# Toeplitz weights of a state-space layer, copied on GpSimd into contiguous columns before the products load them

## The chip, the cores and the metric

The kernel runs on one core of one Trainium2 chip. The metric is the device time of one execution in microseconds (us). The engines are named as in the profile: PE is TensorE (matrix products), PEld its weight loads, DVE is VectorE, ACT is ScalarE, POOL is GpSimd, SP is SyncE, which here only issues transfers.

## The reference, cut to what matters

One layer of a hybrid decoder for 512 prompt positions and 8 sample tokens. The part that the change touches is the state-space mixer: 32 groups of 16 channels, each with 64 complex states.

```python
bu = jnp.einsum('bcgi,gpi->bcgp', u_c, b_bar)            # inputs into the states
_, local = lax.associative_scan(combine, (a, bu), axis=1)  # s[t] = lam_bar * s[t-1] + bu[t]
s_all = local + decay[None] * s[:, None]
y = jnp.einsum('bcgp,gip->bcgi', s_all, c_mat).real      # states out to the channels
...
y = y.reshape(bsz, t, D_SSM) + ssm_d * u_f
out = z * sigmoid(z @ w_glu)                              # z = gelu(y)
```

Around it stand the modulation (`w_ada`), the input projection (`w_in`), three attention branches, the output projection (`w_out`) and an MLP of width 4096. All of it is float32.

## The kernel before, in words

The kernel writes the scan in steps of 8 positions. Within a step the output of a group is a lower triangular block Toeplitz product of its inputs (8 positions x 16 channels = 128 rows); across the 64 steps it is a scan over the carried state. The loop `for qd in range(8)` handles a **quad** of 4 groups at a time:

- `BP`, `Cb` (DVE) are the powers of lambda times B and C. `pm0` (L766, PE) is the 16-column kernel of each group, copied to `M0` (L768, DVE; the trace calls these `pm` and `M`).
- `M0` is written to DRAM (`mscr`, L772) and read back with overlapping rows as the Toeplitz block `Tz` (L774), a tile of [128, 8, 16, 4]: position, channel and, innermost, the group. The columns of one group so lie 4 floats (16 bytes) apart. Both transfers are issued by SP.
- `pvs` (L792, PE) takes the inputs into the states; `Vs`, `Vp` (ACT), `W`, the scan `Rr` (L803, DVE) and `Rp` (ACT) lead to `Sx` (DVE and two small POOL memsets, L808 and L813). `rho` (L785) is the scan's decay, copied on POOL.
- `py` (named `pys`) adds two products for each group: one with weights `Tz` (L819) and one with weights `Cb` (L820).

```python
for g in range(GQ):
    c = slice(g * 80, (g + 1) * 80)
    nc.tensor.matmul(py[:, c], Tz[:, :, :, g].rearrange("p t c -> p (t c)"), U[:, qd * GQ + g], start=True, stop=False)
    nc.tensor.matmul(py[:, c], Cb[:, g].rearrange("p t c -> p (t c)"), Sx[:, g, 0:80], start=False, stop=True)
```

A float32 product of this kind appears as two records (two passes) in the trace, so 32 products of a line are 64 records.

All tiles of the loop have one buffer. Beside the loop stand other products, which the same stretch holds: the compressed keys of the samples (`turned`: `pxc`, `xc`; `compressed`: `ph`, `pk`, `php`), the modulation (`pada`, `padt`) and the key and value projections (`pkv`). A scheduler sets the order of instructions on every engine from a model of their durations; each engine then works through its own list strictly in order. So a change of one instruction can move others, also far behind it. The attention stage that follows (`pst` scores, `pe` exponentials, `ptp` and `PT` transposes, `po` values; `rslc` gathered cache rows, `pkT`, `ktS`, `poS` for the samples) is ordered in the same way; there `w_out` (`wo`) is loaded and split by ACT (L63) and DVE (L64).

Of the kernel before, what the change touches and what calls it, by code (L numbers as in the profile page):

```python
# [9 lines left out]
F32 = mybir.dt.float32  # L10
# [6 lines left out]
P = 128  # L17
# [19 lines left out]
def body(tc, i, o, dbg=None):  # L37
    nc = tc.nc
# [18 lines left out]
    def pst(tag, name):  # L57
        return bank["tile"].tile([P, 512], F32, tag=tag, name=name, bufs=bank["tags"][tag])
# [154 lines left out]
    GQ = 4  # L213
# [271 lines left out]
    def cmul(outr, outi, ar_, ai_, br_, bi_, tmp):  # L485
        nc.vector.tensor_tensor(outr, ar_, br_, ALU.mult)
        nc.vector.tensor_tensor(tmp, ai_, bi_, ALU.mult)
        nc.vector.tensor_tensor(outr, outr, tmp, ALU.subtract)
        nc.vector.tensor_tensor(outi, ar_, bi_, ALU.mult)
        nc.vector.tensor_tensor(tmp, ai_, br_, ALU.mult)  # L490
        nc.vector.tensor_tensor(outi, outi, tmp, ALU.add)
# [102 lines left out]
    sl = slx.enter_context(tc.tile_pool(name="sl", bufs=1, reuse_waits="tile"))  # L594
    xTp = sl.tile([P, 2, 2, 8, 32], F32, name="xTp")
    U = sl.tile([P, NG, 80], F32, name="U")
# [130 lines left out]
    for qd in range(NG // GQ):  # L727
# [43 lines left out]
        Tz = sl.tile([P, 8, 16, GQ], F32, tag="Tz", name="Tz")  # L771
        nc.sync.dma_start(mscr[qd, 112:240], M0.rearrange("p c g -> p (c g)"))  # L772
        mw = mscr[qd, 0:P]
        nc.sync.dma_start(Tz, bass.AP(tensor=mw.tensor, offset=mw.offset, ap=[[GQ * 16, P], [16 * GQ * 16, 8], [1, GQ * 16]]))  # L774

        CT = sl.tile([P, GQ, 8, 8], F32, tag="CT", name="CT")
        ST = sl.tile([P, GQ, 8, 8], F32, tag="ST", name="ST")
        tq = sl.tile([P, GQ, 8, 8], F32, tag="tq", name="tq")
        b8 = [P, GQ, 8, 8]
        ab = [tab[:, x, 1, gs].unsqueeze(3).to_broadcast(b8) for x in range(2)] + [tab[:, x, 0, gs].unsqueeze(2).to_broadcast(b8) for x in range(2)]  # L780
        cmul(CT, ST, *ab, tq)
        CT = CT.rearrange("p g a b -> p g (a b)")
        ST = ST.rearrange("p g a b -> p g (a b)")
# [14 lines left out]
        W2 = sl.tile([P, GQ, 64], F32, tag="W2", name="W2")  # L798
        nc.vector.tensor_tensor(W, Vs[:, :, 0:64], CT, ALU.mult)
        nc.vector.tensor_tensor(W2, Vp, ST, ALU.mult)  # L800
# [8 lines left out]
        nc.vector.tensor_tensor(W2, Rp, ST, ALU.mult)  # L809
        nc.vector.tensor_tensor(W, Rr, CT, ALU.mult)  # L810
        nc.vector.tensor_tensor(Sx[:, :, 1:65], W, W2, ALU.subtract)
# [4 lines left out]
        py = pst("ss", "pys")  # L816
        for g in range(GQ):
            c = slice(g * 80, (g + 1) * 80)
            nc.tensor.matmul(py[:, c], Tz[:, :, :, g].rearrange("p t c -> p (t c)"), U[:, qd * GQ + g], start=True, stop=False)  # L819
            nc.tensor.matmul(py[:, c], Cb[:, g].rearrange("p t c -> p (t c)"), Sx[:, g, 0:80], start=False, stop=True)  # L820
        nc.scalar.copy(ys.rearrange("p g c -> p (g c)"), py[:, 0 : GQ * 80])
        nc.sync.dma_start(yscr[qd], ys)
# [482 lines left out]
    for n in range(16):  # L1305
# [6 lines left out]
        if n % 4 == 3:  # L1312
            nc.tensor.matmul(po, Vbd[:, j // 2, 2 * (j % 2) : 2 * (j % 2) + 2].rearrange("p h d -> p (h d)"), etc[:, j // 2], start=False,
                             stop=True)
# [265 lines left out]
```

## Time and profile before

| | |
|---|---|
| times of three runs, us | 912.84, 912.87, 920.48 (median 912.87) |
| the profiled execution, us | 918.94; its span 917.2 |
| PE busy, share of the span | 95% |
| DVE, ACT, POOL busy | 58%, 42%, 7% |
| state-space loop in the span | about 133 to 264 us |
| attention | about 265 to 456 us |
| output projection and MLP | from about 456 us to the end |

The busy share of PE is made of modelled ends, so the rows are read by the starts of instructions that follow each other. The profiled execution is 6.07 us above the median of the three runs; a term worked out from it is taken off either.

### The profile page before, as it was taken

How to read it: one execution, taken by the hardware profiler on the slowest of the kernel's cores; microseconds unless marked ns; L12 is line 12 of the kernel's file. 1: busy time of each engine (PE TensorE's matmuls, PEld its weight loads, DVE VectorE, ACT ScalarE, POOL GpSimd, SP SyncE). 2: the span in 40 equal slices, each digit the busy share in tenths (PEclk: the TensorE clock that was granted, in tenths of full speed). 3: DMA queues.
4: the chain of work that ended last, by engine and by line, in shares of the span. 5: the costliest groups of instructions: out<-in, count | busy, mean ns of one | idle time of the engine just before them, and what ended most of it. 6: DMA issues, size and time to landing. Idle time of an engine off the chain costs nothing.

```text
span 917.2 us, 16412 instructions
## 1 busy us (share of the span) xinstructions
PE 869.2 (95%) x6517; PEld 759.1 (83%) x6517; DVE 527.5 (58%) x1413; ACT 388.7 (42%) x880; POOL 65.1 (7%) x147
## 2 busy tenths in 40 slices
PE   2899999999999999997999999999999999999995
PEld 1667997788998566655669989999999999999995
DVE  5776564758847865565659875443333444434534
ACT  1555325534435655454646544442111344433322
POOL 6001101000144100000000000000000000000000
PEclk9999997999999999997999999999999999999998
DMA  8957587366465352104154572233332222332302
GB/s 290 322 173 246 188 149 216 116 207 192 119 205 170 106 183 92 40 8 184 43 189 134 188 231 66 95 87 91 94 90 92 91 93 93 88 97 80 93 1 94
DMA packets 111836, 122.36 MB, mean 133 GB/s; under 512 B 24500, under 2 KB 91880, under 8 KB 109584
## 3 DMA queue, kind: packets, MB, share of 16 engines
q1 hardware_dynamic: 102256, 89.71, 32.2%
q0 software_dynamic: 5488, 29.99, 9.6%
q10 hardware_dynamic: 4016, 1.62, 0.7%
q8 instruction: 51, 0.84, 0.4%
q14 instruction: 25, 0.20, 0.1%
HBM read 112.47 MB, written 13.03 MB: 137 GB/s over the span
## 4 chain that ended last, share of the span: by engine, by line
PE 87%; DMA 7%; ACT 3%; DVE 2%; issue 1%; SPq 0%; ACTq 0%
PE pdn L1385 20%; PE pup L1385 20%; PE pj L605 5%; PE pkv L647 5%; PE pwo L1385 5%; PE ph L387 5%; DMA wada<-w_ada 4%; PE po L1244 4%; PE pada L334 2%; PE ptp L1239 2%; PE pg L1261 2%; PE pys L819 2%; PE pst L1211 1%; PE pS L1032 1%; PE pkT L1023 1%; PE pst L1212 1%
## 5 line engine op out<-in xcount | busy, mean ns | idle before, releaser
L1385 PE MATMUL pdn<-hidL,wH 128*128 128x256 f32 (+1 forms) x480 | 136.1, 284 | 0.0
L1385 PE MATMUL pdn<-hidH,wL 128*128 128x256 f32 (+1 forms) x480 | 135.9, 283 | 0.0
L1385 PE MATMUL pdn<-hidH,wH 128*128 128x256 f32 (+1 forms) x480 | 135.4, 282 | 0.0
L1385 PE MATMUL pup<-h2H,wL 128*128 128x256 f32 (+1 forms) x480 | 135.0, 282 | 0.0
L1385 PE MATMUL pup<-h2L,wH 128*128 128x256 f32 (+1 forms) x480 | 135.0, 282 | 0.0
L1385 PE MATMUL pup<-h2H,wH 128*128 128x256 f32 (+1 forms) x480 | 134.1, 283 | 0.0
L1385 PEld LDWEIGHTS pup<-h2L,wH 128*128 128x128 f32 x480 | 90.4, 188 | 0.8 <-DVE rs_t L97 0.8
L1385 PEld LDWEIGHTS pdn<-hidH,wL 128*128 128x128 f32 x480 | 90.6, 189 | 0.0
L1385 PEld LDWEIGHTS pdn<-hidL,wH 128*128 128x128 f32 x480 | 90.4, 188 | 0.1
L1385 PEld LDWEIGHTS pup<-h2H,wL 128*128 128x128 f32 x480 | 90.4, 188 | 0.0
L1385 PEld LDWEIGHTS pdn<-hidH,wH 128*128 128x128 f32 x480 | 90.4, 188 | 0.0
L1385 PEld LDWEIGHTS pup<-h2H,wH 128*128 128x128 f32 x480 | 89.6, 188 | 0.0
L63 ACT CAST wH<-wdn 128x1024 fp32r<-128x1024 f32 x30 | 31.5, 1050 | 114.0 <-PE pdn L1385 104.2
L64 DVE TENSOR_TENSOR wL<-wup,wH 128x1024 fp32r<-128x1024 f32 x30 | 36.7, 1225 | 58.1 <-ACT wH L63 58.1
L64 DVE TENSOR_TENSOR wL<-wdn,wH 128x1024 fp32r<-128x1024 f32 x30 | 36.8, 1225 | 54.2 <-ACT wH L63 54.2
L387 PE MATMUL ph<-xc,w 128*128 128x256 f32 (+2 forms) x320 | 66.4, 360 | 0.7 <-DVE xc L377 0.7
L387 PEld LDWEIGHTS ph<-xc,w 128*128 128x128 f32 x320 | 53.7, 206 | 11.7 <-issue 5.7
L63 ACT CAST wH<-wup 128x1024 fp32r<-128x1024 f32 x30 | 31.5, 1050 | 48.3 <-PE pup L1385 37.6
L1244 PE MATMUL po<-PT,Vx 128*64 128x512 f32 (+3 forms) x128 | 43.9, 450 | 1.5 <-ACT PT L1242 1.5
L1217 DVE TENSOR_REDUCE mxa<-pst 128x1 f32<-128x512 f32 (+1 forms) x64 | 29.7, 486 | 27.1 <-PE pst L1213 27.0
L1463 ACT ACTIVATE rl<-pup 128x256 f32<-128x256 f32 (+1 forms) x64 | 24.4, 384 | 48.9 <-PE pup L1385 48.8
L375 ACT COPY xc<-pxc 64x256 f32<-64x256 f32 x96 | 32.1, 366 | 25.1 <-DVE xc L377 18.6
(557 smaller groups left out, 2032.5 us busy)
## 6 DMA issues: line engine op xcount, KB each, us to landing
wada<-w_ada SPq DMA_DIRECT2D x20, 1024.0 KB
wup<-w_up SPq DMA_DIRECT2D x16, 1024.0 KB
wdn<-w_down SPq DMA_DIRECT2D x16, 1024.0 KB
wo<-w_out SPq DMA_DIRECT2D x8, 1024.0 KB
wada<-w_ada SPq DMA_DIRECT2D x8, 512.0 KB
rwin<-state_win SPq DMA_DIRECT2D x4, 1024.0 KB
new_win_sample<-state_win POOLq DMA_DIRECT2D x2, 2044.0 KB, 8.4
wkv<-w_in SPq DMA_DIRECT2D x3, 1024.0 KB
```

The lines of the kernel that those rows point to most:

```text
L63: nc.scalar.copy(h, src)
L64: nc.vector.tensor_tensor(l, src, h, ALU.subtract)
L334: nc.tensor.matmul(ps[k % 4 * 32 : k % 4 * 32 + 32], cT[:, k], rs[k // kp][:, k % kp], start=(k < 4), stop=(k >= 4))
L375: nc.scalar.copy(dst[:, :, :, hf], srcv[:, :, :, hf])
L387: nc.tensor.matmul(phv[:, lo:hi, 0:w], w1[n][:, r_], xc[n][:, lo:hi, r_ % 8, off : off + w], start=(r_ == 0), stop=(r_ == 15))
L605: nc.tensor.matmul(ps[:, 0:HB], w[:, k], x[:, k, hc], start=(k == 0 and n == 0), stop=(k == KT - 1 and n == 2))
L647: nc.tensor.matmul(ps[0:mp, 0:nw], x[:, k, tok], w[:, k % 4], start=(k == 0 and n == 0), stop=(k == KT - 1 and n == 2))
L819: nc.tensor.matmul(py[:, c], Tz[:, :, :, g].rearrange("p t c -> p (t c)"), U[:, qd * GQ + g], start=True, stop=False)
L1217: nc.vector.tensor_reduce(mx[:, qt : qt + 1], d, AX.X, ALU.max, negate=True)
L1244: nc.tensor.matmul(po[hh * 64 : hh * 64 + 64, kt * P : T], Vx[:, kt, kb], PT[:, c0 : c0 + T - kt * P], start=(br == 0 and kt == 0), stop=F ...
L1385: nc.tensor.matmul(ps[:, 0 : b - a], w, x[:, a:b], start=first and n == 0, stop=last and n == 2)
L1463: nc.scalar.activation(rl, ps[:, 0 : b - a], AF.Relu)
```

## The change: what it does, and the diff

A new tile `Tc` of [128, 4, 128] holds the four blocks of a quad one behind the other. One POOL copy of 512 elements in each of 128 partitions fills it from `Tz`, and the products take their weights from `Tc`. Nothing is removed.

```diff
         nc.sync.dma_start(Tz, bass.AP(tensor=mw.tensor, offset=mw.offset, ap=[[GQ * 16, P], [16 * GQ * 16, 8], [1, GQ * 16]]))
 
+        Tc = sl.tile([P, GQ, P], F32, tag="Tc", name="Tc")
+        nc.gpsimd.tensor_copy(Tc, Tz.rearrange("p t c g -> p g (t c)"))
+
...
         for g in range(GQ):
             c = slice(g * 80, (g + 1) * 80)
-            nc.tensor.matmul(py[:, c], Tz[:, :, :, g].rearrange("p t c -> p (t c)"), U[:, qd * GQ + g], start=True, stop=False)
+            nc.tensor.matmul(py[:, c], Tc[:, g], U[:, qd * GQ + g], start=True, stop=False)
```

In the changed kernel the lines behind L775 stand three lower (L819 is L822, L820 is L823, L785 is L788); the copy is L777.

The scheduler's order changes with it, from the first `pys` to the end of attention; the output projection and the MLP keep theirs. Three places follow.

POOL, from the `xc` memset (between the first and the second quad) on, before:

```order
L356 MEMSET xc 128x16x4
L785 COPY rho<-rh_133 128x256
L786 MEMSET rho 128x4
L813 MEMSET Sx 128x4x8
L808 MEMSET Sx 128x4
```

And after:

```order
L356 MEMSET xc 128x16x4
L777 COPY Tc<-Tz 128x512
L788 COPY rho<-rh_133 128x256
L789 MEMSET rho 128x4
L816 MEMSET Sx 128x4x8
L811 MEMSET Sx 128x4
```

The copy of each quad stands ahead of the next quad's `rho` copy and of this quad's `Sx` memset, so both wait until `Tz` has landed and been copied.

PE, from the last product of the first quad to the first Toeplitz product of the second, before (`w_155` and `w_156` are the two halves of the compression weights, `pm_1644`, `pm_1646` and so on a quad's `pm0`):

```order
L820 MATMUL pys<-Sx,Cb 128x80
L792 MATMUL pvs<-U,Bb 128x72 x4
L387 MATMUL ph<-xc,w_155 128x2x128 x7
L387 MATMUL ph<-xc,w_156 128x2x128 x6
L819 MATMUL pys<-U,Tz 128x80
```

And after:

```order
L823 MATMUL pys<-Sx,Cb 128x80
L766 MATMUL pm_1646<-C_136,BP 128x16 x4
L387 MATMUL ph<-xc,w_155 128x2x128 x5
L387 MATMUL ph<-xc,w_156 128x2x128 x3
L767 MATMUL pbb<-ident,BP 128x128 x4
L387 MATMUL ph<-xc,w_156 128x2x128 x11
L795 MATMUL pvs<-U,Bb 128x72 x4
L387 MATMUL ph<-xc,w_156 128x2x128
L822 MATMUL pys<-U,Tc 128x80
```

The second quad's `pm0`, which before stood ahead of these rows, behind the first Toeplitz product, has moved into this piece: 4 `pm`, 20 `ph`, 4 `pbb` and 4 `pvs` now lie between it and the product that needs its block.

ACT, in attention, from a value copy to the score exponentials, before:

```order
L1050 COPY ptS<-ppt 128x512 x2
L1221 ACTIVATE pe,dn<-pst,mxa 128x512
L1125 ACTIVATE ovS<-poS,sdn 128x128
L1270 COPY bcr<-bc 128x512
L1271 COPY bcr<-bs 128x8
L63 CAST wH<-wo 128x1024 x2
L1221 ACTIVATE pe,dn<-pst,mxa 128x128
```

And after:

```order
L1053 COPY ptS<-ppt 128x512 x2
L1245 COPY PT<-ptp 128x512 x2
L1128 ACTIVATE ovS<-poS,sdn 128x128
L1245 COPY PT<-ptp 128x256
L1224 ACTIVATE pe,dn<-pst,mxa 128x512
L63 CAST wH<-wo 128x1024
L1273 COPY bcr<-bc 128x512
```

The cast of `wo` stands a few rows earlier among the copies, and still ahead of the next exponentials.

## Rows read from the trace of the kernel before

**Rows 1.** Busy time by stage: stretch; its us; PE, PEld, DVE, ACT, POOL busy; clock.

```profile
144.00:265.00 121.00, 120.43 (x821) 107.34 (x820) 82.99 (x224) 52.07 (x141) 13.29 (x40) 0.96 0.53 164
265.00:417.00 152.00, 149.61 (x983) 101.23 (x981) 95.92 (x282) 81.30 (x218) 24.02 (x55) 1.00 0.33 108
417.00:426.00 9.00, 2.95 (x17) 2.39 (x17) 6.21 (x12) 3.89 (x9) 0.93 (x1) 0.68 0.90 345
```

**Rows 2.** The chain of waits from 140 to 270 us, by line (cut by the view).

```profile
by line: PE ph L387 22.5%; PE pkv L647 22.4%; PE pys L819 10.6%; PE pada L334 6.6%; PE php L697 5.5%; PE pys L820 5.4%; PE pm L766 4.3%; DMA wada<-w_ada 4.2%; PE pxc L368 4.1%; PE pvs L792 4.0%; ACT xc L375 3.5%; PE pbb L767 2.7%; PE padt L
```

**Rows 3.** The instructions of `pys`: ns minimum/median/maximum, first and last start, form.

```profile
L819 PEld LDWEIGHTS pys<-U,Tz x64: 308/326/337, 144.4 to 262.5; 128*128 128x128 f32 x64
L820 PEld LDWEIGHTS pys<-Sx,Cb x64: 187/190/208, 154.0 to 262.9; 128*128 128x128 f32 x64
```

**Rows 4.** PE in order of time, first quad: start, us, line, operation.

```profile
154.38 0.63 PE L819 MATMUL pys<-U,Tz 128*128 128x80 f32 x2
154.84 0.39 PE L820 MATMUL pys<-Sx,Cb 128*128 128x80 f32 x2
155.06 0.63 PE L819 MATMUL pys<-U,Tz 128*128 128x80 f32 x2
```

**Rows 5.** PE, a quad's first Toeplitz product and what follows, twice.

```profile
162.99 0.48 PE L819 MATMUL pys<-U,Tz 128*128 128x80 f32 x2
163.30 4.52 PE L387 MATMUL ph<-xc,w 128*128 128x256 f32 x20
...
177.06 0.64 PE L819 MATMUL pys<-U,Tz 128*128 128x80 f32 x2
177.53 1.04 PE L368 MATMUL pxc<-ident,rc 128*128 128x128 f32 x8
```

**Rows 6.** POOL in order of time: a memset of 512 elements and `rho` copies of 256.

```profile
95.12 0.54 POOL L719 MEMSET U<- 128x512 f32 x1
96.27 0.40 POOL L785 COPY rho<-rh 128x256 f32<-128x256 f32 x1 [0.60 <-DVE hL L201]
...
228.29 2.07 POOL L785 COPY rho<-rh 128x256 f32<-128x256 f32 x1 [5.99 <-DVE Rr L803]
```

**Rows 7.** DVE in order of time, beside the last of these copies.

```profile
228.35 0.42 DVE L810 TENSOR_TENSOR W<-Rr,CT 128x256 f32<-128x256 f32 x1
...
229.69 0.42 DVE L488 TENSOR_TENSOR CT<-CT,tq 128x256 f32<-128x256 f32 x1
230.02 0.30 DVE L341 TENSOR_REDUCE mod<-padt 128x36 f32<-128x144 f32 x1
```

**Rows 8.** SP's issues of the block's two transfers.

```profile
168.91 0.33 SPq L772 DMA_DIRECT2D mscr<-M  x1
172.25 0.37 SPq L774 DMA_DIRECT2D Tz<-mscr  x1
...
236.26 0.37 SPq L774 DMA_DIRECT2D Tz<-mscr  x1
```

**Rows 9.** PE in order of time: the product behind the last of these, and a row of `ph`.

```profile
157.32 5.82 PE L387 MATMUL ph<-xc,w 128*128 128x256 f32 x26
...
240.92 0.57 PE L819 MATMUL pys<-U,Tz 128*128 128x80 f32 x2
```

**Rows 10.** DVE in order of time, behind the end of a quad's `pys`.

```profile
156.64 0.69 DVE L757 TENSOR_TENSOR Cb<-lr,C 128x512 f32<-128x512 f32 x1 [6.05 <-PE pys L820]
...
157.36 0.69 DVE L759 TENSOR_TENSOR Cb<-Cb,tmp 128x512 f32<-128x512 f32 x1
```

**Rows 11.** The stop in attention, in order of time: transfer, ACT, PE.

```profile
415.66 11.52 SPq L1401 DMA_DIRECT2D wo<-w_out  x2
...
422.75 1.99 ACT L63 CAST wH<-wo 128x1024 fp32r<-128x1024 f32 x2 [5.11 <-DMA wo<-w_out]
...
425.71 0.80 PE L1211 MATMUL pst<-KH,QS 128*128 128x512 f32 x1 [4.02 <-ACT pe L1221]
```

**Rows 12.** PE's other wait of that stretch, 400 to 456 us: us in total, times, longest.

```profile
PE pkT L1023 <- DVE Os L1066: 2.0, 1, 2.0
```

## The prediction

> **What bounds the kernel now.** I read the windows by stage first. Through the state-space loop PE is busy for 120.43 of 121.00 us [rows 1], so it has half a microsecond of idle time there, while DVE, ACT and POOL each have 38 us or more to spare. The chain of waits says the same from the other side: from 140 to 270 us it runs through PE's lines, one behind the other, with transfers at 4.2% and ACT's copies at 3.5% [rows 2]. In such a stretch a shorter PE instruction is worth its own shortening, as long as PE finds its next operand ready. Two shares of that row belong to the edit: the 32 products with `Tz` hold 10.6%, the 32 with `Cb` 5.4%. They have the same shape (128x128 weights, 80 moving columns) and differ in how the weights lie. In attention PE is nearly full as well (149.61 of 152.00 us), but then comes a hole: 2.95 us of work in the 9 us from 417, with the granted clock at 0.68, a mean of its two levels of 2.4 and 1.2 GHz [rows 1]. That hole matters because the change re-orders the instructions around it.
>
> **Removed: the strided weight loads.** A load from `Tz` takes 326 ns, one from `Cb` 190 [rows 3]. Loads overlap with products, so I price by starts. A `Tz` product is followed after 0.46 us (154.38 to 154.84), a `Cb` product after 0.22 (154.84 to 155.06) [rows 4]. Within a quad three of four Toeplitz products stand between `Cb` products: 24 in all, and with contiguous weights each should move at `Cb`'s pace: 24 x (0.46 - 0.22) = 5.8 us. The first product of each quad is followed by something else after 0.31 to 0.47 us [rows 5]; at the middle, 0.39, that is 8 x (0.39 - 0.22) = 1.4 us. Sum 7.2. The chain gives nearly the same: 10.6% less 5.4% of 130 us is 6.8 us [rows 2]. Bounds: 5.8 if the firsts gain nothing, and 64 x 0.136 = 8.7 if each record's whole excess counts [rows 3]. I take 7.0, between the two ways of counting.
>
> **Added: eight copies on POOL.** The trace has no POOL copy of 512 elements or of this stride. Nearest are a memset of 512, 0.54 us, and the `rho` copy of 256, 0.40 [rows 6]. Undisturbed, the new copy is bounded by 0.54 below (a write of as many elements) and, with twice the `rho` copy raised by the stride's factor on PE (326/190 = 1.7), by 1.4 above. I take 0.8, twice `rho`. It can also be held up: the `rho` copy at 228.29 took 2.07 us, and in that time DVE ran one two-input operation after another from 228.35 until a one-input reduction at 230.02 [rows 6, 7]. So a POOL copy that meets such a train can lose 1.7 us; the new one would then take 2.5, or 4.1 if it stretched in proportion. The Trainium skill, "SBUF — State Buffer", section "Who interferes with whom", says that a DVE instruction with two SBUF inputs contends with a GpSimd instruction that reads SBUF, and that the later one waits; these rows agree, and by that rule a copy could also hold up DVE for its own length. By its own 0.8 us that would be 6.4 us of DVE time in eight quads, which DVE has.
>
> None of this is PE time; the question is whether PE has other work until `Tc` is ready. PE does, by its list: after the first quad the next Toeplitz product stands behind 4 `pm`, 20 `ph`, 4 `pbb` and 4 `pvs`. A `ph` record is 5.82/26 = 0.22 us and each `ph` has two, so the `ph` alone cover 9.0 us [rows 9]; the 12 others hold 4.3, 2.7 and 4.0% of the chain's 130 us for eight quads, 1.8 us in one [rows 2]. Cover: 10.8. Against it stands the chain of the block, which in this quad starts late: behind the end of `pys` DVE has two operations on `Cb` and one on `Sx`, from 156.64 to 158.05, 1.4 us [rows 10], and I allow 0.4 (an estimate: a little over half of one 0.69 us operation, for a copy of an eighth of the elements) for `M0` and the way to `mscr`. From the issue of `mscr` to that of `Tz` 3.34 us pass [rows 8]; `Tz` has landed at most 4.66 us after its issue, since the product at 240.92 did not wait [rows 8, 9]. With the copy of 0.8: 1.4 + 0.4 + 3.3 + 4.7 + 0.8 = 10.6, just under the cover; with a copy of 2.5 it is 12.3, over it by 1.5; at 4.1 by 3.1. This is the tightest quad: in the others more rows lie between `pm` and the product. I take 0.5 us of new waiting for this quad and 0.5 for the other seven together, with bounds of 0 and 8 x 3.1 = 25 us.
>
> **Queues that the copy stands in.** POOL's list is in order: while the copy waits for `Tz`, the next quad's `rho` and this quad's `Sx` memset wait with it. `rho` is needed by the next scan, a whole quad later; the `Sx` memset feeds the `Cb` products, which stand behind the Toeplitz product anyway. So I price this at nothing. If the block came later than the scan's result, the memset would be late by the same amount as `Tc`, a wait already counted. In exchange `Tz` is free once it is copied, not once PE is done with it, so SP can issue the next read earlier; a gain of slack, not of time.
>
> **Moved: everything up to 456 us.** The re-ordering keeps the instructions, and PE's own work with it; what can change is where PE waits. The one large stop is at 417 to 426: `wo` is issued at 415.66, lands at 422.75, and ACT, whose next instruction is its cast, stands still for 5.11 us; behind the cast wait the exponentials, and PE stops for 4.0 and 2.0 us [rows 11, 12]. In the new order the cast still stands ahead of the next exponentials, with a few more copies done before it. So I expect the stop to stay: 0, with bounds of -6 (both waits gone; a little more with the clock) and +6 (another such stop).
>
> **The sum.** -7.0 + 1.0 + 0 = -6.0 us. On the profiled execution: 918.94 - 6.0 = 912.9. It is 6.07 above the median of the runs shown, so against the median of 912.87 the forecast is 906.9. Its own range, from the bounds of the loads and half of attention's either way, is 901 to 911.
>
> **The rivals.** *(a) The stop in attention shrinks too.* For: ACT has more copies behind it when it reaches the cast, so PE has more to do meanwhile. Against: `wo` waits for the same buffer and shares its transfer time with two gathers. With both waits gone: -7 + 1 - 6 = -12, 900.9; from -3 on it is faster by over 1%.
>
> *(b) PE waits for the copy in every quad.* Mechanism: DVE's two-input trains hold up the POOL copy (2.07 us instead of 0.40, [rows 6, 7]), at each `Tc`, and PE reaches the product first. It needs a copy of over 1.0 us in the second quad (cover 10.8, chain 9.8 without the copy) and as little cover in the others. At copies of 4.1 us, 3.1 of waiting in each quad: +25 - 7 = +18, 930.9. From 0.9 us a quad on the gain is eaten, from 2.0 on it is slower by over 1%. For: DVE is busy for 83 of 121 us [rows 1], mostly with such operations. Against: only one of eight `rho` copies shows it at this size, and later quads have more cover.
>
> *(c) The load does not follow the stride.* Then the weights from `Tc` load no faster, and -7.0 falls away: 912.87 + 1.0 = 913.9. For it: the 326 ns could belong to something else about `Tz`. Against: `Cb`'s loads, of the same shape and in the same stretch, never go above 208, and `Tz`'s never below 308 [rows 3]. The Trainium skill, "TensorE: Matmul & The Clock Gate", section "LDWEIGHTS (loading the stationary operand)", has the load's time follow from its columns alone, 128 / 1.2 = 107 ns, without a term for stride; by that rule the change saves nothing, and the two medians for the same 128 columns speak against it.
>
> *(d) The new order makes another stop in attention:* +6 - 6 = 0, 912.9.
>
> **How the numbers follow.** Forecast 0.55, (a) 0.20, (b) 0.08, (c) 0.06, (d) 0.11. One per cent (9.1 us) is about what a measurement of this kernel can tell from no change. Faster by over 1% (below 903.7): all of (a) but a quarter, and a little over a fifth of the forecast's own range, 0.15 + 0.12 = 0.27. Slower by over 1%: (b), with 0.01 for a larger stop in (d), 0.09. The rest, 0.64, is within 1%. For 8 in 10 the range reaches from most of (a), 898, to past (c) and (d), 917; (b) is left out above and the end of (a) below.
>
> **What would show it.** Right: loads of `pys` from `Tc` at about 190 ns, `Tc` products followed after 0.22 us, PE idle under 2 us in the loop, POOL copies at 0.6 to 1.4 us with a few longer. Wrong: a wait of PE for POOL at L822, or, behind 265 us, a stop that is new or gone, which would be the larger part of the difference.

## The result, and the profile after

The changed kernel takes 927.65 us (median of 4 runs, 925.1 to 928.6) and the kernel before 914.16 beside it (4 runs). The ratio is 1.0137, 95% interval 1.0099 to 1.0175: 13.5 us slower, where 6 us faster was forecast. The profiled execution took 928.6 us. Two of all the executions timed below, one of e10 at 969.37 us and one of the kernel before at 1407.8 us beside e13, ran at a much lower granted clock (0.847 and 0.562) and stand in no median or ratio here. Of the changed kernel's page, the span, and busy time and instructions by engine:

```profile
span 926.9 us, 16416 instructions
PE 869.2 (94%) x6517; PEld 750.0 (81%) x6517; DVE 534.3 (58%) x1413; ACT 388.2 (42%) x880; POOL 75.9 (8%) x155
```

PE is busy for as long as before, 869.2 us, though its weight loads have become cheaper: the sum also holds products that ran at the lower clock and so took longer, and does not show the saving. Busy time and clock by stage, as in [rows 1], with attention cut where it now stops:

```profile
144.00:265.00 121.00, 116.00 (x841) 99.11 (x839) 89.53 (x224) 52.53 (x143) 17.76 (x38) 0.99 0.52 158
265.00:327.00 62.00, 59.01 (x399) 42.58 (x396) 43.79 (x120) 33.32 (x89) 25.39 (x58) 1.00 0.56 181
327.00:340.00 13.00, 6.21 (x26) 5.09 (x25) 3.94 (x10) 2.37 (x6) 0.00 (x0) 0.74 0.48 158
340.00:417.00 77.00, 76.54 (x416) 46.03 (x415) 41.89 (x125) 39.59 (x110) 2.86 (x3) 1.00 0.12 42
417.00:440.00 23.00, 19.81 (x159) 13.63 (x159) 14.15 (x45) 8.76 (x21) 1.88 (x2) 0.85 0.50 183
```

Two things are new: 5.0 us of idle PE time in the loop (0.57 before), and a hole from 327 to 340 us in which PE does 6.2 us of work in 13, at a mean clock of 0.74. The stop for `wo` is still there, behind 417, and smaller (3.2 us of idle PE time from 417 to 440, 6.1 before). The instructions of `pys`, to be held against [rows 3]:

```profile
L822 PEld LDWEIGHTS pys<-U,Tc x64: 186/192/192, 149.7 to 266.6; 128*128 128x128 f32 x64
L823 PEld LDWEIGHTS pys<-Sx,Cb x64: 188/192/317, 150.0 to 266.8; 128*128 128x128 f32 x64
```

A load from `Tc` takes 192 ns where one from `Tz` took 326. The same group in the view by line and form (busy us, mean ns, idle time before it), of the kernel before:

```profile
L819 PE MATMUL pys<-U,Tz 128*128 128x80 f32 x64 | 19.6, 388 | 0.0
```

and of the changed kernel:

```profile
L822 PE MATMUL pys<-U,Tc 128*128 128x80 f32 x64 | 12.3, 274 | 0.3 <-POOL Tc L777 0.3
```

So the removed cost is gone: 19.6 - 12.3 = 7.3 us, and PE waits for a copy once, for 0.3 us. The copies on POOL, in order of time (the brackets are idle time):

```profile
143.60 1.10 POOL L777 COPY Tc<-Tz 128x512 f32<-128x512 f32 x1
...
215.91 1.65 POOL L777 COPY Tc<-Tz 128x512 f32<-128x512 f32 x1 [7.60 <-DMA Tz<-mscr]
```

The time must be lost elsewhere. PE's waits in the loop, 144 to 270 us (us in total, times, longest):

```profile
PE pada L334 <- DMA wada<-w_ada: 1.7, 1, 1.7
PE pxc L368 <- ACT xc L375: 1.5, 1, 1.5
PE pkv L647 <- ACT kvs L650: 0.7, 1, 0.7
```

These are other work's waits; none has to do with `Tz` or `Tc`. And this is the hole in attention, in order of time over all engines:

```profile
319.30 1.08 PE L1124 MATMUL poS<-rwin,ptS 128*32 128x128 f32 x32
319.60 0.68 POOL L280 DMA_DIRECT2D new_win_sample<-state_win  x1 [0.18 <-issue]
320.40 0.39 SPq L1153 DMA_DIRECT2D rwin<-state_win  x1
320.72 1.65 POOL L159 DMA_INDIRECT rslc<-cache_slc,pidx  x1 [0.44 <-PE poS L1124]
...
327.66 0.33 PE L1130 MATMUL pov<-ident,ovS 128*128 128x128 f32 x1
334.77 1.09 PE L1026 MATMUL pkT<-ident,rwin 128*128 128x128 f32 x4 [6.79 <-DMA rwin<-state_win]
...
340.17 1.05 PE L1035 MATMUL pS<-ktS,q 128*32 128x512 f32 x4
```

The samples' window attention reads `state_win` through `rwin` tiles of 1 MB. The fourth needs a buffer that is free once PE has done the `poS` products of the first. In the new order these come at 319.30, the transfer is issued at 320.40, and PE stands before the first transpose of that tile from 327.98 to 334.77, which is 14.4 us after the issue. Around it two more transfers are issued on POOL: a copy of 2 MB from `state_win` to the output `new_win_sample`, and a gather. The same place in the kernel before:

```profile
321.05 0.53 POOL L280 DMA_DIRECT2D new_win_sample<-state_win  x1 [0.18 <-issue]
...
330.57 0.39 SPq L1150 DMA_DIRECT2D rwin<-state_win  x1
...
331.76 1.03 POOL L159 DMA_INDIRECT rslc<-cache_slc,pidx  x1 [10.18 <-PE poS L1121]
...
335.93 1.04 PE L1023 MATMUL pkT<-ident,rwin 128*128 128x128 f32 x8
```

There the `poS` products were spread among other rows and ended at 331; the 2 MB copy (8.0 us to landing) was over when the `rwin` transfer was issued, and the second half of the row at 335.93, which reads that tile, waited for nothing. What the transfers of 319 to 335 us moved after the change (total, then KB each):

```profile
DMA packets 496, 4.19 MB, mean 262 GB/s; under 512 B 48, under 2 KB 48, under 8 KB 304
...
new_win_sample<-state_win POOLq DMA_DIRECT2D x1, 2044.0 KB
rwin<-state_win SPq DMA_DIRECT2D x1, 1024.0 KB
rslc<-cache_slc,pidx POOLq DMA_INDIRECT x1
```

All three run together. And the clock behind the stop (stretch; its us; PE, PEld, DVE, ACT, POOL busy; clock):

```profile
330.00:333.00 3.00, 0.00 (x0) 0.00 (x0) 0.23 (x1) 0.00 (x0) 0.00 (x0) 0.99 0.87 345
333.00:335.00 2.00, 0.23 (x1) 0.26 (x2) 0.00 (x0) 0.00 (x0) 0.00 (x0) 0.50 0.20 82
...
338.00:339.00 1.00, 1.00 (x5) 0.70 (x4) 0.00 (x0) 0.47 (x2) 0.00 (x0) 0.50 0.00 0
339.00:340.00 1.00, 1.00 (x8) 1.00 (x6) 0.67 (x1) 0.53 (x2) 0.00 (x0) 0.62 0.08 16
```

PE resumes at its lower level of 1.2 GHz and stays there until 339 us.

### The profile page after: what moved, and what is told of

Its sections match the earlier page's. It is cut to its first block, busy times and chain, and to the rows that moved or that the text cites. A ratio compares the mean times of both kernels' runs of the same rounds, so it can differ in the third digit from the quotient of the medians.

```text
span 926.9 us, 16416 instructions
## 1 busy us (share of the span) xinstructions
PE 869.2 (94%) x6517; PEld 750.0 (81%) x6517; DVE 534.3 (58%) x1413; ACT 388.2 (42%) x880; POOL 75.9 (8%) x155
## 4 chain that ended last, share of the span: by engine, by line
PE 79%; DMA 11%; DVE 4%; ACT 4%; issue 1%; SPq 0%; POOL 0%; ACTq 0%; DVEq 0%
PE pdn L1388 20%; PE pup L1388 20%; PE pj L605 5%; PE pwo L1388 5%; DMA wada<-w_ada 4%; PE ph L387 4%; PE po L1247 4%; PE pada L334 2%; PE pkv L647 2%; PE ptp L1242 2%; PE pS L1035 2%; DMA rwin<-state_win 2%; PE pst L1214 1%; PE pkT L1026 1%; PE pg L1264 1%; DMA mscr<-M 1%
## 5 line engine op out<-in xcount | busy, mean ns | idle before, releaser
L387 PE MATMUL ph<-xc,w 128*128 128x256 f32 (+2 forms) x320 | 64.5, 352 | 1.1 <-DVE xc L377 0.7
```

The source lines that it names most:

```text
L387: nc.tensor.matmul(phv[:, lo:hi, 0:w], w1[n][:, r_], xc[n][:, lo:hi, r_ % 8, off : off + w], start=(r_ == 0), stop=(r_ == 15))
```

## The experiments

**Theory A:** the loads save what was forecast, and the order that the scheduler wrote for the change costs more. **Theory B:** the copy itself, or the waits for it, cost the time. To part them, some kernels are held in a given order: behind the body, instructions of each engine that follow each other in a table get an edge that orders their issue and waits for nothing else. The table is read from the built program whose order is wanted; the copies into `Tc` are not in it.

```diff
+        for p, q in zip(seq, seq[1:]):   # seq: one engine's instructions in the wanted order
+            tc.add_manual_dep(q, p.name, mb.DependencyInfo(mb.DependencyClass.NoSync, mb.DependencyReason.DATA), reason="order")
...
         body(tc, i, o)
+        pin_order(tc, ORDER)
```

**e1: the loads alone.** On the kernel before:

```diff
-            nc.tensor.matmul(py[:, c], Tz[:, :, :, g].rearrange("p t c -> p (t c)"), U[:, qd * GQ + g], start=True, stop=False)
+            nc.tensor.matmul(py[:, c], Tz.rearrange("p t c g -> p (t c g)")[:, g * P : (g + 1) * P], U[:, qd * GQ + g], start=True, stop=False)
```

> The kernel before, with one edit: the Toeplitz products take 128 columns that lie side by side in Tz (of a mixed group of columns, so these products' values are not the reference's); there is no copy and no Tc, and every engine's order is that of the kernel before. Theory A (the order that the scheduler wrote costs the time; the loads themselves save what was forecast): 7 us less than the kernel before, 905 to 908 us. Theory B (the saving of the loads is lost anyway, since other work in the loop sets the end there): within 2 us of the kernel before.

913.86 us (12 runs), ratio 0.997, 0.9935 to 1.0005. By the median it is within 2 us of the kernel before, as theory B has it; by the ratio it is 2.7 us less, and the interval reaches from 6 us less to no change. So it is not decided: see e8 and e12.

**e2: the change in the old order.** The changed kernel with the table of the kernel before.

> The changed kernel with every instruction of every engine held in the order of the kernel before; only the copies find their own places on GpSimd. Theory A (the order costs the time): 905 to 910 us, that is the forecast of 906.9 within the waits for the copy. Theory B (the copy and the waits for it cost the time, wherever they stand): 920 us or more, with idle time of TensorE before the Toeplitz products in most quads.

916.19 us (12 runs), ratio 1.0009, 0.9974 to 1.0043. Neither hit: the loss is gone, and so is the gain. PE and POOL in order of time:

```profile
146.57 0.71 PE L822 MATMUL pys<-U,Tc 128*128 128x80 f32 x2 [2.33 <-POOL rho L789]
...
177.52 0.45 PE L822 MATMUL pys<-U,Tc 128*128 128x80 f32 x2 [1.02 <-POOL Tc L777]
...
226.15 2.68 POOL L777 COPY Tc<-Tz 128x512 f32<-128x512 f32 x1 [6.35 <-DMA Tz<-mscr]
...
228.88 0.45 PE L822 MATMUL pys<-U,Tc 128*128 128x80 f32 x2 [1.99 <-POOL Tc L777]
```

In the old order PE does wait for copies, at three quads and for 5.3 us together (at the first, the copy ends at 146.52; the `rho` named there is POOL's next instruction). In the changed kernel's own order 0.3 us of this is left.

**e3: the kernel before in the new order.** The table of the changed kernel, no other edit.

> The kernel before (strided weights, no copy) with every instruction of every engine held in the order of the changed kernel. Theory A (the order costs the time): as slow as the changed kernel and slower by the loads, 927 to 936 us, with a stop of 4 to 8 us of TensorE before the transposes of the fourth rwin tile. Theory B (the copy costs the time): 912 to 915 us.

934.88 us (6 runs), ratio 1.0205, 1.0164 to 1.0245, with 6.7 us of waiting for `rwin`. Theory A: the order alone costs 15 to 22 us, and in it the loads and copies save 934.88 - 927.65 = 7.2. (By the two ratios it is 6.2; with intervals of about 4 us either way on each, the saving is known to some 5 us.)

**e4: the copies alone.**

```diff
-            nc.tensor.matmul(py[:, c], Tc[:, g], U[:, qd * GQ + g], start=True, stop=False)
+            nc.tensor.matmul(py[:, c], Tz[:, :, :, g].rearrange("p t c -> p (t c)"), U[:, qd * GQ + g], start=True, stop=False)
```

> The changed kernel, but the Toeplitz products still take their strided weights from Tz: the copies are made and nothing reads them. The order is that of the kernel before but for 31 of TensorE's instructions, which move by a few places. Theory A: the copy by itself costs next to nothing, within 2 us of the kernel before. Theory B (GpSimd's copies hold up VectorE or the rho and Sx steps behind them): 5 us or more over the kernel before.

914.79 us (12 runs), ratio 0.9996, 0.9965 to 1.0027. Copies that nobody waits for cost nothing that can be measured, though one of them took 2.98 us. And since only 31 of TensorE's instructions move here, against 1299 in the changed kernel, it is the products' dependence on `Tc` that re-orders the kernel.

**e5 and e6: half of each order.** The changed kernel; the cut is the loop's last Toeplitz product, e5 with the new order ahead of it and the old one behind, e6 the other way round.

> The changed kernel, with what stands up to the last Toeplitz product of the loop in the changed kernel's order and what stands behind it in the order of the kernel before. Theory A (the larger part of the order's price lies in attention, at the stop before the transposes of the fourth rwin tile, 6.8 us of waiting and 6 us of half clock behind it): 915 to 921 us, no wait for rwin over 2 us. Theory C (the price lies in the loop's new order, at its stops between 168 and 174 us and the half clock behind them): 924 us or more.

> The changed kernel, with what stands up to the last Toeplitz product of the loop in the order of the kernel before and what stands behind it in the changed kernel's order. Theory A: 923 to 930 us, with 6 to 8 us of waiting for rwin before the transposes of its fourth tile. Theory C: 914 to 918 us.

e5: 917.68 us (10 runs), ratio 1.005, 1.002 to 1.008. e6: 929.57 us (4 runs), 1.0174, 1.0131 to 1.0217. The price lies behind the loop. PE's largest wait in e6:

```profile
PE pkT L1026 <- DMA rwin<-state_win: 7.0, 1, 7.0
```

**e7: the old order from the stop on.** The cut of e5, moved to the first transpose of the fourth `rwin` tile.

> The changed kernel in its own order up to the place at which TensorE stops for rwin; from there on what is left stands in the order of the kernel before, so that other work stands between the issue of the fourth rwin transfer and its first transpose. Theory A (that one stop, with the half clock behind it, is 9 to 11 us): 915 to 920 us. Theory D (the stop takes only the place of other waits, and attention in the new order loses the time elsewhere): 923 us or more.

917.78 us (10 runs), ratio 1.0036, 1.0002 to 1.0070: theory A. From that place on the old order is 9.9 us cheaper, and it is as cheap as the old order throughout (e2, within the intervals). The trace adds a point:

```profile
317.82 0.68 POOL L280 DMA_DIRECT2D new_win_sample<-state_win  x1 [0.18 <-issue]
318.63 0.39 SPq L1153 DMA_DIRECT2D rwin<-state_win  x1
...
332.94 1.04 PE L1026 MATMUL pkT<-ident,rwin 128*128 128x128 f32 x8
```

The fourth `rwin` transfer is issued as early here as in the changed kernel, and the 2 MB copy stands as close ahead of it. But PE has other work and comes back to transposes of `rwin` 14.3 us behind the issue, and it does not wait. So two things must meet for the stop: a transfer that is late, and too little other work ahead of the product that needs it.

**e8: the loads alone again,** one more execution of the program of e1.

> The same program as the run with the loads alone, for a second profile: its twelve times fell in two groups, near 908 and near 915 us, and the first profile is one of the faster group. If this one is of the slower group, its trace shows what the group pays: theory A expects a stretch at half clock more than in the first profile, behind a wait in the loop or in the adaLN products, and not a longer weight load.

911.93 us, between the groups. The half clock is there, but in two places: in the loop the mean clock is 0.97 against 0.99 in e1, and the stop for `wo` is longer. That stop in e1, whose profiled run took 907.57 us:

```profile
405.22 10.11 SPq L1401 DMA_DIRECT2D wo<-w_out  x2
...
410.90 1.99 ACT L63 CAST wH<-wo 128x1024 fp32r<-128x1024 f32 x2 [3.70 <-DMA wo<-w_out]
...
413.86 0.80 PE L1211 MATMUL pst<-KH,QS 128*128 128x512 f32 x1 [2.60 <-ACT pe L1221]
```

and in e8:

```profile
407.32 13.11 SPq L1401 DMA_DIRECT2D wo<-w_out  x2
...
416.00 1.99 ACT L63 CAST wH<-wo 128x1024 fp32r<-128x1024 f32 x2 [6.70 <-DMA wo<-w_out]
...
418.96 0.79 PE L1211 MATMUL pst<-KH,QS 128*128 128x512 f32 x1 [6.06 <-ACT pe L1221]
```

The same transfer lands 5.7 us after its issue in one run and 8.7 in the other. The times of one program spread by several us, and they go with the mean granted clock of the execution: of the 12 runs of e1, the three below 908 us had 0.986 to 0.993, and the two above 916.5 us 0.984 and 0.979. This limits what a single run or trace can tell.

**e9: one instruction moved.** The changed kernel in its own order; in POOL's row of the table the second 2 MB copy stands three gathers later.

Of that row, the end ([n, k] stands for k instructions from number n on; 130 is the copy, 134, 136 and 138 are the gathers):

```diff
-[126, 5], [134, 1], [136, 1], [138, 5]
+[126, 4], [134, 1], [136, 1], [138, 1], [130, 1], [139, 4]
```

> The changed kernel in its own order, with one instruction moved on GpSimd's queue: the second copy of 2 MB from state_win to new_win_sample (the transfer issued at 319.60 us) stands behind the third gather after it, which comes at 353.7 us, so that it no longer runs beside the fourth rwin transfer. Theory A, sharpened (the stop is a collision: the new order frees rwin's buffer 11 us earlier, and its transfer then shares the engines with the 2 MB copy): the wait for rwin falls from 6.8 to 2 us or less, no half clock behind it, 917 to 920 us. Theory E (the transposes simply come too early behind the release of the buffer, or the gather beside it is the heavier load): a wait of 4 us or more stays, 923 us or more.

917.56 us (10 runs), ratio 1.0029, 1.0001 to 1.0057: 10.1 us less than the changed kernel. In order of time:

```profile
318.92 0.39 SPq L1153 DMA_DIRECT2D rwin<-state_win  x1
319.24 1.64 POOL L159 DMA_INDIRECT rslc<-cache_slc,pidx  x1 [1.31 <-PE poS L1124]
...
326.18 0.33 PE L1130 MATMUL pov<-ident,ovS 128*128 128x128 f32 x1
326.35 0.60 PE L1026 MATMUL pkT<-ident,rwin 128*128 128x128 f32 x4
...
329.81 1.05 PE L1035 MATMUL pS<-ktS,q 128*32 128x512 f32 x4
```

The gather still runs beside it, the transposes still come 7.4 us after the issue, and there is no wait. From `pov` to `pS` PE takes 3.6 us, where the changed kernel took 12.5: 8.9 of the 10.1 us in this one place, 6.8 of them waiting and 2.1 mostly the half clock. The collision is shown, and theory E falls: with the early release and the gather as they were, the wait is gone.

**e10: the first product from `Tz`, in the old order.** It reads `Tz`, as before, and has no copy to wait for:

```diff
-            nc.tensor.matmul(py[:, c], Tc[:, g], U[:, qd * GQ + g], start=True, stop=False)
+            nc.tensor.matmul(py[:, c], Tc[:, g] if g else Tz[:, :, :, 0].rearrange("p t c -> p (t c)"), U[:, qd * GQ + g], start=True, stop=False)
```

> The changed kernel in the order of the kernel before, and the first of the four Toeplitz products of a quad takes its strided weights from Tz, as before; the three others take theirs from Tc. Theory A (in the old order it was the wait for Tc at the first product, 5.3 us in three places, that ate the gain): no wait for Tc over 0.5 us, the 24 other products at 0.22 us, and 3 to 6 us less than the changed kernel in the old order: 910 to 913 us. Theory F (the copies themselves cost, by what they take from VectorE and GpSimd): 915 us or more.

912.73 us (11 runs), ratio 0.9968, 0.9944 to 0.9991: theory A. PE no longer waits for `Tc`; one line of its waits names `pys`:

```profile
PE pys L822 <- DMA Tz<-mscr: 1.2, 1, 1.2
```

**e11: the same in its own order.**

> The same edit as in the run before, but with the order that the scheduler writes for it: on TensorE 642 of 5771 instructions stand elsewhere than in the kernel before, none ahead of the second quad's copies; behind the release of rwin's buffer 21 rows of other work stand ahead of the waiting transposes, where the changed kernel has 10 and the kernel before 18 to 29. Theory A (the order at the rwin transposes decides): a wait for rwin between 0 and 4 us, 911 to 918 us. Rival (any order but the old one costs 10 us or more): 922 us or more.

915.68 us (12 runs), ratio 1.0007, 0.9980 to 1.0034, with one wait for `rwin` of 4.3 us, just past the expected 4. Not every new order costs 10 us.

**e12: the loads alone, timed again.** No edit to e1.

> The program with the loads alone once more, timed beside the others, since its interval against the kernel before reached from 6 us less to no change. Theory A (the saved 7 us of TensorE reach the end, less what the stop for wo gives back in some executions): 2 to 6 us less than the kernel before. Theory B (all of it is given back): within 1 us of the kernel before.

910.63 us (12 runs), ratio 0.9941, 0.9916 to 0.9966: theory A. By the ratios of e1 and e12 the loads are worth some 3 to 5 us at the end in the old order, not all of the 7.3. The trace, of an execution of 913.91 us, does not bear out that the stop for `wo` gives back the rest: there PE waits 2.8 us for the exponentials, less than in the kernel before (4.5) or in e1 (3.1). Among its waits in the loop are 1.4 us for `Tz` itself, and the clock is 0.81 from 226 to 235 us, behind that wait.

**e13: e3 with the copy moved.** The kernel before, new order, the edit of e9.

> The kernel before (strided weights, no copy into Tc) in the changed kernel's order, with the second 2 MB copy moved behind the third gather, as in the run that moved it for the changed kernel. Theory A (the collision is one term of the order's price, about 10 us, whatever the weights): 10 us less than the same kernel without the move (934.9), 923 to 927 us, and what is left over the kernel before, 9 to 12 us, is the price of the rest of the new order. Theory G (the collision was the whole price, and strided weights only move it): 914 to 918 us.

927.0 us (4 runs, 919.8 to 929.85), ratio 1.0145, 1.0106 to 1.0184: 7.9 us less than e3 by the medians, 5.5 by the ratios, where theory A had 10; and it is still 11 us above the kernel before. The trace has no wait for `rwin`, where e3 has 6.7 us. The collision is one term of the order's price; the rest of the order costs the old kernel at least as much again.

**e14: the loads alone in the new order.**

> The loads alone (128 columns of Tz that lie side by side, of a mixed group, so these products' values are not the reference's; no copy) in the changed kernel's order. Theory A (in the new order the copy costs next to nothing, since TensorE waits for Tc once and for 0.3 us): within 2 us of the changed kernel, 925 to 929 us, with the same stop for rwin. Theory F (the copies cost through GpSimd and VectorE): 920 to 924 us.

925.6 us (4 runs), ratio 1.0105, 1.0067 to 1.0144, and 6.8 us of waiting for `rwin`: 2.1 us less than the changed kernel by the medians, 2.9 by the ratios. This is in the range of theory A (925 to 929), and a price of the copies of 2 or 3 us in the new order cannot be told from none with four runs.

**e15: e11 with the copy moved.**

> The kernel whose first Toeplitz product of a quad reads Tz, in the order that the scheduler wrote for it, with the second 2 MB copy moved behind the third gather after it. Its wait for rwin was 4.3 us. Theory A (the same collision): that wait is gone, with the half clock behind it, and the time falls from 915.7 by 4 to 7 us, to 909 to 912 us, under both kernels. Rival (the wait is the gather's or comes from elsewhere): within 2 us of 915.7.

909.87 us (12 runs), ratio 0.9956, 0.9928 to 0.9984: 5.8 us less than e11, and faster than both kernels. PE's largest waits between 90 and 480 us, with `rwin` no longer among them:

```profile
PE pst L1214 <- ACT pe L1224: 2.4, 2, 2.1
PE pkT L1026 <- DVE Os L1069: 2.0, 1, 2.0
PE pada L334 <- DMA wada<-w_ada: 1.6, 2, 1.0
```

## Why the prediction was wrong

| | old order | new order | new order, 2 MB copy moved |
|---|---|---|---|
| strided weights, no copies | 914.35 (before) | 934.88 (e3) | 927.0 (e13) |
| contiguous, no copies | 913.86, 910.63 (e1, e12) | 925.6 (e14) | |
| contiguous, copies (the change) | 916.19 (e2) | 927.65 | 917.56 (e9) |

The cells are medians in us, of sets of runs timed at different times. The kernel before came out between 913.6 and 915.7 in these sets, and e1 and e12, one program, 3.2 apart; a difference between two cells is known to some 3 us, and to some 5 where a cell has four to six runs.

*Removed, -7.0: right in mechanism and size on PE.* The loads fell to 192 ns and the products' busy time by 7.3 us, so rival (c) is out. The rule of the Trainium skill, "TensorE: Matmul & The Clock Gate", section "LDWEIGHTS (loading the stationary operand)", which has no term for stride, does not hold here: 326 ns against 192 for the same 128 columns. But PE's busy time is not the kernel's: 6 to 7 us reach the end in the new order, the copies included (e3 to the change), 3 to 5 in the old one. In the expectation of e12 I put the rest down to the stop for `wo`; the rows do not show that. The issue of `wo` moves up with the loop (415.66 before; 405.22, 407.32 and 411.40 in e1, e8 and e12), and only in e8 is the stop longer than before. Part of the rest is idle time in the loop, 0.9, 1.8 and 3.1 us in the traces of e1, e8 and e12 against 0.57 before; where all of it goes stays open.

*Added, +1.0: right in kind, the parts mis-sized.* I costed it in the new order, and there PE waits 0.3 us, in one quad. I took a copy at 0.8 us, bounds 0.54 to 1.4; it takes 1.10 to 1.65. The cover in the second quad came out as priced, but the chain was shorter: from the end of `pys` at 151.87 to the end of the copy (157.79 and 1.29) it took 7.2 us, not 10.6, so a copy longer than the 1.0 us of rival (b) still did not hold PE up. In the old order PE would have waited 5.3 us in three quads (e2); the longest copy there, 2.68 us, is near the 2.5 that I gave a copy beside DVE's two-input operations, and DVE ran such operations from 226.14 on. Rival (b) is out in the form I gave it.

*Queues, 0: right.* e4 holds the copies on POOL, and neither PE nor DVE waits for POOL in its loop.

*Moved, 0 with bounds of -6 to +6: the step that failed.* I read the new order only at the old stop, and expected it to stay, which it did. I did not ask of the rows that moved which of them free a buffer, which transfer that starts, and what it then runs beside. The issue of the `rwin` transfer, which waits for that release, moved up by 10 us (330.57 to 320.40), ahead of the end of the 2 MB copy. The bound "+6, another such stop" had the kind of thing right and the size wrong: 10.1 us by e9, since behind the wait comes work at half clock. Rival (a), the old stop getting smaller, came true in part: PE is idle for 3.2 us behind 417 now, 6.1 before. Rival (d), at 0.11, paired it with the full saving; what came is a larger stop.

*A second step failed with it: that in the loop a shorter PE instruction is worth its own shortening.* Without the collision the change is not 6 us faster than the kernel before but 2.8 slower (e9, 0 to 5 by its interval), so some 9 us of the miss are not the stop's. PE's idle time in the loop, which I put under 2 us, is 5.0 in the changed kernel and 4.8 in e9 (2.4 in e3, with the same order and strided weights). Part of it are waits for `xc` and `wada` that end at 170.00 and 172.35; behind them, from 172 to 176, the clock is 0.57 in the changed kernel, and 1.00 in the trace of e9. So part of the saving turns into waits for other work's operands, which the kernel before hardly has (0.57 us of idle time). I had made the saving depend on PE finding its next operand ready, and asked that of `Tc` alone. The old loop order does not keep it either: there the waits are for `Tc` (e2). So the loop's order by itself is worth no more than a few us (e5 against e2, e6 against the change), within the spread.

The new order could be read beforehand. PE between the release of the buffer and the first transposes that need it, after the change:

```
L1124 MATMUL poS<-rwin,ptS 32x128 x16
L1026 MATMUL pkT<-ident,rwin 128x128 x4
L1242 MATMUL ptp<-ident,pe 128x128 x4
L1247 MATMUL po<-PT,Vx 64x512
L1242 MATMUL ptp<-ident,pe 128x128 x2
L1126 MATMUL poS<-kvs,pnw 32x128 x4
L1264 MATMUL pg<-uT,wglu 128x260 x4
L1247 MATMUL po<-PT,Vx 64x384
L1247 MATMUL po<-PT,Vx 64x128
L1264 MATMUL pg<-uT,wglu 128x260 x2
L1247 MATMUL po<-PT,Vx 64x256
L1130 MATMUL pov<-ident,ovS 128x128
L1026 MATMUL pkT<-ident,rwin 128x128 x4
```

That is 7.6 us of work (320.40 to 327.98) ahead of a transfer that, started there, cannot be alone: the issue of the 2 MB copy stands at nearly the same time in both kernels (319.60 and 321.05). The last line of the prediction did name what came, a new stop behind 265 us as the larger part of the difference. It stood there as a sign; its price, in rival (d), was that of the old stop.

Still open: without the collision the new order costs the old kernel 11 us more (e13 against the kernel before), the changed one 1.4 (e9 against e2). The waits for the copy, which the old order has (5.3 us in the trace of e2), would make up about half of that difference. For the rest of the 11 us the trace of e13 is no witness: it is of the fastest of four executions, 919.8 us at a mean clock of 0.996, and the three others took 924.97 to 929.85 at 0.984 to 0.990. A place where they may have lost it is seen in e3, whose clock is 0.67 from 168 to 180 us, behind the new order's waits in the loop, where the trace of e13 has 1.00; for those three executions this is not shown. Nor does anything here tell why `wo` lands after 5.7 us in one run and 8.7 in another: the same two gathers are issued beside it in both.

## What to carry to other kernels

When a scheduler re-orders around a change, look in the new order for the last readers of each buffer that a transfer waits for: if they move up, the transfer moves up too, and may meet another one that it used to follow. Hold the old order to learn what a change is worth by itself; here it parted +1.8 us of edit (known to some 3) from +11.5 of order (to some 5). Such a stop can be mended from either side: keep the two transfers apart (e9), or leave PE enough other work behind the issue (e7). And where a copy feeds several products, let the first read the original: that took some 3 us off in the old order (e10 against e2), and with one transfer moved, in its own order, gave 909.87 us (e15).

## What the runs showed of the hardware

- A 1 MB transfer issued within a microsecond of a 2 MB copy and a gather on GpSimd's queues landed 14.4 us after its issue in the changed kernel and 14.3 to 14.5 in e3, e11 and e14; without the 2 MB copy it was ready within 7.4 (e9). The Trainium skill, "DMA: Bandwidth & Descriptors", section "Queues, rings and completion order", says that an engine takes turns between the queues that have work for it; these rows fit that, without showing the turns themselves.
- The granted clock fell while PE was idle (0.99 from 330 to 333 us, 0.50 in the next stretch) and PE then worked at the lower level for over 4 us: the same instructions from the first transposes to `pS` took 5.4 us, and 3.5 in e9.
- A GpSimd copy of 128x512 that reads at a 16-byte stride took 1.08 to 1.65 us in most cases and up to 2.98 (e2, e4), against 0.40 to 0.66 for most of the `rho` copies of 256 beside it.
